# Joining small products and transposes on TensorE's queue in a two-block transformer kernel, and putting products of one PSUM bank ahead of its first reading

## The chip, the core and the metric

The kernel runs on one core of one Trainium2 chip. The metric is device time in microseconds of the whole program, the median of three runs. TensorE's clock has two levels, 1.2 and 2.4 GHz; the profile gives the granted share of the higher one.

## What is computed

Two transformer blocks one after the other on 256 tokens of width 1024, in float32. Cut to what matters here:

```
# first block, two layers l = 0, 1 (shared keys and values come in at l = 1)
proj = rmsnorm(h) @ w_in[l]                    # 768 columns "main", 256 "memory queries"
main_out = pool_mixer(main)          (l = 0)   # windowed means, then 4 groups of 192x192 weights
         = sliding_window_attn(...)  (l = 1)   # 12 heads of 64
mem_out  = softmax(q . mk) @ mv                # 4 heads of 64 over 256 memory rows
h += concat(main_out, mem_out) @ w_out[l]
h += relu(rmsnorm(h) @ w_up)**2 @ w_down       # 4096 wide
# second block
hq, hf, hi, hg, aq, ak, av, gl = split(rmsnorm(x) @ w_in)
y_hg = gated linear recurrence over time       # 8 heads of 128, within 128-token tiles by levels
y_at = causal attention with a bias            # 8 heads of 128
x += (gate0 * y_hg + gate1 * y_at) @ w_out;  x += silu-gated MLP(x)
```

## The kernel before

**Tiles.** The 256 tokens are two tiles `tt` of 128 rows. A weight product is three float32r products (high x high, high x low, low x high; tiles `wh`, `wl`, `xh`, `xl`), since weights and activations are split in a rounded part and a rest. In the rows `wh,xh` of 512 columns is such a product. What belongs to attention, pooling and the recurrence is done in plain float32; the profile records each plain product twice, so that "x4" of them are two products, and a transpose once.

**Order.** `Line` is a small planner in the kernel: every strand of work is a generator with a rank, which yields a latency in microseconds (or an event) whenever its next step must wait for another engine, and `Line.run` lets other strands, mostly weight products in pieces of six, fill the time. The framework's scheduler then places the instructions of each engine, keeps a bank's reader and the products written to the same bank apart by semaphores, and rotates four banks named `mm` and four named `acc`.

**The array's shapes.** A plain product whose contraction or output has 64 rows or fewer runs in a part of the array: in the profile `64*128` (64 rows contracted), `128*64` (64 output rows), `64*64` or `128*32` in place of `128*128`. Two products in different parts of the array can run side by side.

**Places that the change touches.** In stage mix0 (40 to 85 us of the span) `pool_mix` (line 917) multiplies six feature tiles `k` by `pool_w`, two tiles to a bank; feature tiles 1 and 4 take part in two groups, so each has 64-row products. `mem_attention` (line 867; also in stage mix1, 298 to 350 us) scores four heads, makes exponentials `me`, transposes them as two halves `i` (`exp_T`, line 441) and multiplies the copies `eT` by the memory values `mv`: a 64-row output each, half `i` in output rows 64i and on, both halves side by side. `Norm.into` (401) and `turned` (508) transpose a tile of 128 tokens as two halves of four transposes. In `mlp`, `turn` and `up_one` (564 to 575) do so for the hidden tile of one token tile. In the second block `on_q` and `diagonal` (1228 to 1247) make the 32x32 blocks on the diagonal, `recurrence` (1301) works by levels (`level`, line 1249: tile `fQ`, `fK`), `heads_T` and `heads_proj` (1370 to 1388) normalise and transpose four heads of queries or keys, and `score` in `attend` (1410) puts two heads' logits into one bank and reads each.

Of the kernel before, what the change touches and what calls it, by code (L numbers as in the profile page):

```python
# [8 lines left out]
F32 = mybir.dt.float32  # L9
# [6 lines left out]
P = 128  # L16
# [25 lines left out]
def kernel(  # L42
# [149 lines left out]
    def col(i, n=1):  # L192
        return cols[:, i:i + n]
# [189 lines left out]
    class Norm:  # L383
# [17 lines left out]
        def into(self, xs, tt, g, done):  # L401

            xn, lat = self.xn, 1.2
            if self.r is None:
                self.rstd()
                lat = 3.0
            else:
                xn = keep.tile([P, D], F32, tag="xn", name="xn", bufs=2)
            for c in range(2):
                V.tensor_scalar(xn[:, half(c)], self.src[:, half(c)], self.r, None, op0=ALU.mult)  # L410
            for c in range(2):
                yield lat
                split_T(xn[:, half(c)], xs, tt, 4 * c, 4, g[:, 4 * c:4 * c + 4])
                lat = 0.8
            done.at(2.0)
# [92 lines left out]
    def turned(xs, src, tt, g, done):  # L508

        for c in range(2):  # L510
            split_T(src[:, half(c)], xs, tt, 4 * c, 4, None if g is None else g[:, 4 * c:4 * c + 4])
            yield 1.3
        done.at(1.5)

    def add_turned(xs, g=None):

# [36 lines left out]
    def mlp(key, xs, there, nb, ku, hidden, finish, ends=1):  # L553
# [7 lines left out]
            for tt in range(TT):  # L561
                hT_there[b, tt] = Event()

        def turn(b, tt, y):
            yield 3.2
            split_T(y, hT[b], tt, 0, ku)
            hT_there[b, tt].at(5.1)

        def up_one(b, tt):

            if b not in hT:
                hidden_tiles(b)
            ps = mm_bank()
            yield from lin(ps, ktiles(xs, tt), W((key, "up", b)))
            line.add(-2, turn(b, tt, hidden(ps)))

        def up(b):
            hidden_tiles(b)
# [288 lines left out]
    def mem_attention(l, q, xs, tt, q_there, done):  # L867
# [20 lines left out]
        for i, ps in enumerate(pss):  # L888
# [8 lines left out]
            V.reciprocal(sm[:, 2 * i:2 * i + 2], sm[:, 2 * i:2 * i + 2])  # L897
            for hp in range(2):
                scaled(e[i][:, hp, :], sm[:, 2 * i + hp:2 * i + hp + 1])
        yield 3.2  # L900
        eTs = []
        for i in range(2):
            eTs.append(exp_T([e[i][:, hp, tok(c)] for hp in range(2) for c in range(2)]))
            yield 1.5
        po = by128(mm_bank())
        for hp in range(2):
            for c in range(2):
                for i in range(2):
# [8 lines left out]
    def pool_mix(xs, done):  # L917

        a, b = (act.tile([P, 6, S], F32, tag="win", name="win", bufs=2) for _ in range(2))
        prev = u  # L920
        for lev, (k0, s) in enumerate(((0, a), (1, b), (3, a), (4, b))):
            n = 1 << lev
            for eng, t0, t1 in ((V, k0, 5), (G, 5, 6)):
                if t0 < t1:
                    o = slice(t0, t1)
                    eng.tensor_copy(s[:, o, :n], prev[:, o, :n])
                    eng.tensor_tensor(s[:, o, n:], prev[:, o, n:], prev[:, o, :S - n], ALU.add)  # L927
            for k, p0, p1, g in PIECES:
                if g == lev:
                    r, w = s[p0:p1, k, :], WIN[g]  # L930
                    V.tensor_tensor(r[:, :w], r[:, :w], short[p0:p1, g, :w], ALU.mult)  # L931
                    V.scalar_tensor_tensor(u[p0:p1, k, :], r, 1.0 / w, u[p0:p1, k, :], op0=ALU.mult, op1=ALU.subtract)  # L932
            prev = s
        for k0 in range(0, 6, 2):
            yield 6.0 if k0 == 0 else 0
            ps = mm_bank().rearrange("p (k t) -> p k t", t=S)
            for k in (k0, k0 + 1):
                for t, q0, q1, g in PIECES:
                    if t != k:
                        continue  # L940
                    d0 = k * P + q0 - g * 192
                    src = [(t2, r0, r1) for t2, r0, r1, g2 in PIECES if g2 == g]
                    for i, (t2, r0, r1) in enumerate(src):
                        mm(ps[q0:q1, k - k0, :], pw[r0:r1, t2, d0:d0 + q1 - q0], u[r0:r1, t2, :],
                           i == 0, i == len(src) - 1)
                xh, xl = (t[:, k, :] for t in xs)
                A.activation(xh, ps[:, k - k0, :], AF.Copy, scale=col(V_PSCALE + k))
                V.scalar_tensor_tensor(xl, ps[:, k - k0, :], col(V_PSCALE + k), xh.bitcast(F32),
                                       op0=ALU.mult, op1=ALU.subtract)
        done.at(1.5)  # L950

    mem_kv = {0: add_mem_kv(0, 0, 6.0, accs1)}
# [266 lines left out]
    def on_f(c, hs, ps):  # L1219
        A.activation(fF[c][:, hs, :], ps, AF.Sigmoid)  # L1220
        A.activation(fK[c][:, hs, :], ps, AF.Sigmoid, scale=-1.0)
        for i in range(hs.start, hs.stop):
# [2 lines left out]
            V.tensor_scalar(f, f, olb[:, hd:hd + 1], lb[:, hd:hd + 1], op0=ALU.mult, op1=ALU.add)  # L1225
            V.tensor_scalar(k, k, olb[:, hd:hd + 1], None, op0=ALU.mult)

    def on_q(c, hs, ps):
        V.scalar_tensor_tensor(fQ[c][:, hs, :], ps, HG_SCALE, fF[c][:, hs, :], op0=ALU.mult, op1=ALU.mult)
        qs = b2([2, S], "qs")  # L1230
        A.activation(qs, ps, AF.Copy, scale=HG_SCALE)
        line.add(5, diagonal(c, hs, qs))

# [6 lines left out]
    def diagonal(c, hs, qs):  # L1240
        yield 1.5
        pd = mm_bank()[:, :128].rearrange("p (h t) -> p h t", t=32)
        for i in range(2):
            for tt in range(TT):
                quarters(pd[:, 2 * i + tt, :], fK[c][:, hs.start + i, tok(tt)], qs[:, i, tok(tt)], 32)
        V.tensor_tensor(AI[c][:, 2 * hs.start:2 * hs.stop, :], pd, own[:, None, :].to_broadcast([P, 4, 32]), ALU.mult)
        diag_done[c, hs.start].at(2.1)

    def level(m, c):
        def halves(t):  # L1250
# [38 lines left out]
                q = slice(32 * i, 32 * i + 32)  # L1289
                A.copy(at[q, :, q], AI[c][q])  # L1290

    diag_done = {(c, j): Event() for c in range(2) for j in (0, 2)}
    A_there, hv_there = events(), events()

    def gates_T(c):
# [3 lines left out]
        yield from head_chunk("hq", c, on_q)  # L1299

    def recurrence(c):
        yield [diag_done[c, 0], diag_done[c, 2]]
        for m in (1, 2, 4, 8, 16, 32, 64):
            level(m, c)
            yield 6.0
# [61 lines left out]
    q_there, k_there, v_there = events(), events(), events()  # L1367
    left = {}

    def heads_T(t, dst, scale, done):  # L1370

        y = head_norm(t, 4, P, b2([4, P], "hn"))
        yield 8.4
        pt = by128(mm_bank())
        for i in range(4):
            tr(pt[:, i, :], y[:, i, :])
        if scale is None:
            A.copy(dst, pt)
        else:
            A.activation(dst, pt, AF.Copy, scale=scale)  # L1380
        left[done] = left.get(done, 0) + 1
        if left[done] == 2:
            done.at(5.8)

    def heads_proj(key, c, tt, dst, scale, done):
        t = b2([4, P], "tm")
        A.copy(t, by128((yield from project((key, c), x2, tt))))
        line.add(9, heads_T(t, dst, scale, done))

    def attention_in():  # L1390
        for c in range(2):
# [10 lines left out]
    def attend(tt, xs, done):  # L1402
# [7 lines left out]
        def score(hp):  # L1410
            sc = scs[hp] = b2([2, S], "sc")
            ps = acc_bank().rearrange("p (h k) -> p h k", k=S)
            for i in range(2):
                hd = 2 * hp + i
                c = slice(hd, hd + 1)
                mm(ps[:, i, :nk], aq[tt][:, hd, :], ak[hd // 4][:, hd % 4, :nk])
                V.tensor_tensor_reduce(sc[:, i, :nk], ps[:, i, :nk], rel[hd // 4][:, hd % 4, k0:], 1.0, -3 * NEG,
                                       ALU.add, ALU.min, nm[:, c])
                A.activation(sc[:, i, :nk], sc[:, i, :nk], AF.Exp, bias=nm[:, c], scale=-1.0, accum_out=sm[:, c])
# [179 lines left out]
```

## Time and profile before

| | |
|---|---|
| median of three runs | 1031.24 us (1030.45 to 1032.26) |
| the profiled execution | 1031.49 us |
| its span, from first to last instruction | 1029.6 us |
| TensorE busy | 1022.1 us (99%) |
| TensorE's weight loads busy | 901.6 us (88%) |
| VectorE, ScalarE, GpSimd busy | 640.0, 565.4, 100.8 us |
| granted clock over the span | 1.000 |
| HBM read | 182.58 MB |

The median is 0.25 us below the profiled execution, whose time is 1.9 us more than its span. A TensorE record is longer than its share of the time, because products overlap in the array: what a product costs is the distance from its start to the next one's. Such starts are what the rows further down are used for.

### The profile page before, as it was taken

To read this page: it belongs to the slowest core of one execution; us is meant where nothing else is said; L and a number is where in the kernel's file an instruction comes from. 1 tells how busy PE (TensorE), PEld (TensorE's weight loads), DVE (VectorE), ACT (ScalarE), POOL (GpSimd) and SP (SyncE) were. 2 spreads that over 40 slices of the span, in tenths; PEclk is the share of its full clock that TensorE was granted. 3 is DMA by queue.
4 is the path that set the end of the run, shared out by engine and by line. 5 is a ranking of instruction groups with operands and counts; after the bars stand their busy time and mean duration, and the time that the engine had idled before them with its cause. 6 is when DMAs were issued, how large, how long until landed. Compare 5 with 4: busy or idle time off the path is not lost.

```text
span 1029.6 us, 18411 instructions
## 1 busy us (share of the span) xinstructions
PE 1022.1 (99%) x7353; PEld 901.6 (88%) x7353; DVE 640.0 (62%) x1002; ACT 565.4 (55%) x904; POOL 100.8 (10%) x143
## 2 busy tenths in 40 slices
PE   9999999999999999999999999999999999999998
PEld 8768999998876788899988988888999988999997
DVE  6976664565678765564576569847635766455553
ACT  6856544454678654444466455758744455444341
POOL 1524000000142000000000004330000000000000
PEclk9999999999999999999999999999999999999999
DMA  9854566556552269666557554334455566565741
GB/s 339 279 164 163 166 196 208 169 185 207 181 165 82 71 182 327 198 191 212 171 181 237 196 165 165 124 124 156 142 184 175 179 196 199 164 216 167 231 145 41
DMA packets 107765, 186.40 MB, mean 181 GB/s; under 512 B 6808, under 2 KB 31648, under 8 KB 107680
## 3 DMA queue, kind: packets, MB, share of 16 engines
q1 hardware_dynamic: 106160, 180.13, 53.8%
q0 software_dynamic: 1104, 4.80, 1.4%
q8 instruction: 57, 0.93, 0.4%
q10 hardware_dynamic: 416, 0.30, 0.1%
q14 instruction: 28, 0.23, 0.1%
HBM read 182.58 MB, written 2.63 MB: 180 GB/s over the span
## 4 chain that ended last, share of the span: by engine, by line
PE 94%; DVE 2%; DMA 2%; issue 1%; ACT 0%; ACTq 0%
PE acc L152 58%; PE mm L152 33%; PE mm L159 3%; DMA raw<-in_w_mem_kv_dram 1%; DVE wl L248 1%; DMA raw<-in_w_in_dram 1%; DMA raw_T<-in_xT_dram 0%; DVE wl L243 0%; DVE u L932 0%; DVE u L820 0%; DVE hs L427 0%; ACT xn L398 0%; DVE win L931 0%; ACT wh L247 0%; DVE win L927 0%
## 5 line engine op out<-in xcount | busy, mean ns | idle before, releaser
L243 DVE TENSOR_TENSOR wl<-raw,wh 128x1024 fp32r<-128x1024 f32 (+1 forms) x316 | 378.2, 1219 | 174.0 <-ACT wh L242 168.2
L242 ACT CAST wh<-raw 128x1024 fp32r<-128x1024 f32 (+1 forms) x316 | 322.5, 1045 | 171.9 <-PE acc L152 100.0
L152 PE MATMUL mm<-xh,wh 128*128 128x256 f32 x752 | 208.2, 277 | 0.0
L152 PE MATMUL mm<-xl,wh 128*128 128x256 f32 x752 | 207.8, 276 | 0.0
L152 PE MATMUL mm<-xh,wl 128*128 128x256 f32 x752 | 207.7, 276 | 0.0
L152 PEld LDWEIGHTS mm<-xh,wh 128*128 128x128 f32 x752 | 141.2, 188 | 1.4 <-issue 0.4
L152 PEld LDWEIGHTS mm<-xl,wh 128*128 128x128 f32 x752 | 141.3, 188 | 1.0
L152 PEld LDWEIGHTS mm<-xh,wl 128*128 128x128 f32 x752 | 141.2, 188 | 0.0
L152 PE MATMUL acc<-wh,xh 128*128 128x512 f32 x336 | 138.1, 411 | 0.0
L152 PE MATMUL acc<-wh,yl 128*128 128x512 f32 x342 | 134.7, 394 | 0.0
L152 PE MATMUL acc<-wl,yh 128*128 128x512 f32 x342 | 134.0, 392 | 0.0
L152 PE MATMUL acc<-wh,yh 128*128 128x512 f32 x342 | 133.4, 390 | 0.0
L152 PE MATMUL acc<-wh,xl 128*128 128x512 f32 x337 | 132.5, 394 | 0.0
L152 PE MATMUL acc<-wl,xh 128*128 128x512 f32 x336 | 132.1, 393 | 0.0
L152 PE MATMUL acc<-xh,wh 128*128 128x256 f32 x416 | 115.6, 278 | 0.7 <-ACT wh L242 0.7
L152 PE MATMUL acc<-xh,wl 128*128 128x256 f32 x416 | 115.2, 277 | 0.5 <-DVE wl L243 0.5
L152 PE MATMUL acc<-xl,wh 128*128 128x256 f32 x416 | 115.2, 277 | 0.0
L152 PEld LDWEIGHTS acc<-xh,wh 128*128 128x128 f32 x416 | 78.1, 188 | 1.2 <-ACT wh L242 1.1
L152 PEld LDWEIGHTS acc<-xh,wl 128*128 128x128 f32 x416 | 78.1, 188 | 0.9 <-DVE wl L243 0.9
L152 PEld LDWEIGHTS acc<-xl,wh 128*128 128x128 f32 x416 | 78.2, 188 | 0.2
L152 PEld LDWEIGHTS acc<-wl,yh 128*128 128x128 f32 x342 | 64.2, 188 | 13.7
L152 PEld LDWEIGHTS acc<-wh,xh 128*128 128x128 f32 x336 | 63.2, 188 | 14.8 <-issue 2.8
(240 smaller groups left out, 1283.0 us busy)
## 6 DMA issues: line engine op xcount, KB each, us to landing
raw<-in_w_in_dram SPq DMA_DIRECT2D x86, 512.0 KB, 4.7
raw<-in_w_up_dram SPq DMA_DIRECT2D x64, 512.0 KB, 4.7
raw<-in_w_down_dram SPq DMA_DIRECT2D x64, 512.0 KB, 4.8
raw<-in_w_out_dram SPq DMA_DIRECT2D x24, 512.0 KB, 4.8
raw<-in_w_ffn_gate_dram SPq DMA_DIRECT2D x44, 256.0 KB, 4.2
raw<-in_w_ffn_up_dram SPq DMA_DIRECT2D x44, 256.0 KB, 4.6
raw<-in_w_ffn_down_dram SPq DMA_DIRECT2D x22, 512.0 KB, 5.2
raw<-in_w_mem_kv_dram SPq DMA_DIRECT2D x8, 512.0 KB, 10.3
```

The lines of the kernel that those rows point to most:

```text
L152: PE.matmul(out_, lhsT, rhs, start=start, stop=stop)
L159: PE.transpose(out_, in_, ident)
L242: A.copy(wh[:, ks, :], raw[:, ks, :])
L243: V.tensor_sub(wl[:, ks, :], raw[:, ks, :], wh[:, ks, :].bitcast(F32))
L248: V.scalar_tensor_tensor(wl[:, k, :], raw[:, k, :], gk, wh[:, k, :].bitcast(F32), op0=ALU.mult, op1=ALU.subtract)
```

## The change

It moves instructions and adds none: as many products and transposes run on TensorE as before. The edits are these.

- `Norm.into`, `turned`: for token tile 0 the two halves are transposed one right after the other, without a pause for other work; for token tile 1 as before.
- `mlp`: the hidden tiles of two `up_one` calls are transposed together, after the second.
- `mem_attention`: both halves' exponentials are waited for (4.0 us in the plan, before 3.2) and transposed without a pause; among the value products half 1, whose copy is the later one, comes first.
- `pool_mix`: each feature tile has a bank of its own.
- `diagonal`: two pairs of heads go together into one bank, with one multiplication behind them.
- `heads_T`: two projections are normalised first and then transposed together.
- `attend.score`: both heads' products come ahead of the first reading of their bank.

```
@@ Norm.into
             for c in range(2):
-                yield lat
+
+                if tt or c == 0:
+                    yield lat if tt else lat + 0.8
                 split_T(xn[:, half(c)], xs, tt, 4 * c, 4, g[:, 4 * c:4 * c + 4])
@@ turned
             split_T(src[:, half(c)], xs, tt, 4 * c, 4, None if g is None else g[:, 4 * c:4 * c + 4])
-            yield 1.3
-        done.at(1.5)
+            if tt:
+                yield 1.3
+        done.at(2.8 if tt == 0 else 1.5)
@@ mlp
-        def turn(b, tt, y):
+        ys = []
+
+        def turn(ys):
             yield 3.2
-            split_T(y, hT[b], tt, 0, ku)
-            hT_there[b, tt].at(5.1)
+            for b, tt, y in ys:
+                split_T(y, hT[b], tt, 0, ku)
+                hT_there[b, tt].at(5.1)
...
-            line.add(-2, turn(b, tt, hidden(ps)))
+            ys.append((b, tt, hidden(ps)))
+            if len(ys) == 2:
+                line.add(-2, turn(ys[:]))
+                ys.clear()
@@ mem_attention
-        yield 3.2
+        yield 4.0
         eTs = []
         for i in range(2):
             eTs.append(exp_T([e[i][:, hp, tok(c)] for hp in range(2) for c in range(2)]))
-            yield 1.5
+        yield 1.5
         po = by128(mm_bank())
         for hp in range(2):
             for c in range(2):
-                for i in range(2):
+
+                for i in (1, 0):
@@ pool_mix
-        for k0 in range(0, 6, 2):
-            yield 6.0 if k0 == 0 else 0
-            ps = mm_bank().rearrange("p (k t) -> p k t", t=S)
-            for k in (k0, k0 + 1):
...
+        for k in range(6):
+            yield 6.0 if k == 0 else 0
+            ps = mm_bank()[:, :S]
...
@@ on_q, diagonal
-        line.add(5, diagonal(c, hs, qs))
+        qss.append((hs, qs))
+        if len(qss) == 2:
+            line.add(5, diagonal(c, qss[:]))
+            qss.clear()
...
-        V.tensor_tensor(AI[c][:, 2 * hs.start:2 * hs.stop, :], pd, own[:, None, :].to_broadcast([P, 4, 32]), ALU.mult)
-        diag_done[c, hs.start].at(2.1)
+        V.tensor_tensor(AI[c], pd, own[:, None, :].to_broadcast([P, 8, 32]), ALU.mult)
+        diag_done[c].at(2.1)
@@ heads_T, heads_proj
-        line.add(9, heads_T(t, dst, scale, done))
+        ys.append((head_norm(t, 4, P, b2([4, P], "hn")), dst, done))
+        if len(ys) == 2:
+            line.add(9, heads_T(ys[:], scale))
+            ys.clear()
@@ attend.score
             for i in range(2):
                 hd = 2 * hp + i
+                mm(ps[:, i, :nk], aq[tt][:, hd, :], ak[hd // 4][:, hd % 4, :nk])
+            for i in range(2):
+                hd = 2 * hp + i
                 c = slice(hd, hd + 1)
-                mm(ps[:, i, :nk], aq[tt][:, hd, :], ak[hd // 4][:, hd % 4, :nk])
                 V.tensor_tensor_reduce(sc[:, i, :nk], ps[:, i, :nk], rel[hd // 4][:, hd % 4, k0:], 1.0, -3 * NEG,
```

How this moves instructions shows on TensorE's queue at three places. In the order's rows the shape is that of the output; names are the tiles (written <- read).

**Stage mix1, around the memory attention of token tile 0** (`me` exponentials, `mv` memory values, `skT`/`qT`, `sc`, `sv` sliding-window scores, weights and values). Before:

```order
L152 MATMUL mm<-eT,sv 64x128 x2
L159 MATMUL mm<-ident,me 128x128 x2
L152 MATMUL acc<-skT,qT 128x128 x2
L159 MATMUL mm<-ident,me 128x128 x2
L152 MATMUL acc<-wh,xl 128x512
L152 MATMUL acc<-skT,qT 128x128 x2
L152 MATMUL mm<-eT,mv_581 64x128
L159 MATMUL mm<-ident,sc 128x128 x4
L152 MATMUL acc<-skT,qT 128x256 x2
L152 MATMUL acc<-skT,qT 128x128
L152 MATMUL mm<-eT,mv_581 64x128 x7
L159 MATMUL mm<-ident,sc 128x128 x2
```

and now:

```order
L159 MATMUL mm<-ident,me 128x128 x4
L152 MATMUL mm<-eT,sv 64x128 x2
L152 MATMUL acc<-skT,qT 128x128 x2
L152 MATMUL acc<-wh,xl 128x512
L152 MATMUL acc<-skT,qT 128x128 x2
L152 MATMUL acc<-skT,qT 128x256 x2
L152 MATMUL mm<-eT,mv_581 64x128 x8
L159 MATMUL mm<-ident,sc 128x128 x4
L152 MATMUL acc<-skT,qT 128x128 x2
L159 MATMUL mm<-ident,pj 128x128 x2
L159 MATMUL mm<-ident,sc 128x128 x2
```

The eight value products on `mv`, one and seven before, stand together, the eight transposes of `me` lie closer, and the single scores on `skT` have come together in pairs.

**Stage mix0, the pooling products** (`u` pooled inputs, `pw` weights, `mkT`/`mqT` memory scores; each `mm` number is a bank). Before:

```order
L152 MATMUL mm_736<-u_92,pw_96 128x256 x2
L152 MATMUL mm_771<-u_92,pw_96 128x256 x2
L152 MATMUL acc_749<-mkT0_571,mqT_596 128x256
L152 MATMUL acc_750<-mkT0_571,mqT_596 128x256
L152 MATMUL acc_749<-mkT0_571,mqT_596 128x256
L152 MATMUL acc_750<-mkT0_571,mqT_596 128x256
L152 MATMUL mm_780<-u_92,pw_96 64x256 x4
L152 MATMUL acc_804<-mkT0_571,mqT_660 128x256 x2
```

and now:

```order
L152 MATMUL mm_736<-u_92,pw_96 128x256 x2
L152 MATMUL mm_765<-u_92,pw_96 64x256 x2
L152 MATMUL acc_743<-mkT0_571,mqT_596 128x256
L152 MATMUL acc_744<-mkT0_571,mqT_596 128x256
L152 MATMUL acc_743<-mkT0_571,mqT_596 128x256
L152 MATMUL acc_744<-mkT0_571,mqT_596 128x256
L152 MATMUL mm_765<-u_92,pw_96 64x256 x2
L152 MATMUL mm_772<-u_92,pw_96 128x256 x2
L152 MATMUL mm_777<-u_92,pw_96 128x256 x2
L152 MATMUL acc_814<-mkT0_571,mqT_660 128x256 x2
```

Feature tiles 0 and 2, which had the banks 736 and 771 and stood next to each other, are parted: tile 1 (bank 765) and the scores come between them.

**Stage mix0, the memory attention of token tile 0 behind them.** Before:

```order
L159 MATMUL mm<-ident,me 128x128 x4
L159 MATMUL mm<-ident,ks 128x128 x2
L152 MATMUL acc<-mkT_571,mqT 128x256
L152 MATMUL acc<-wh,xh 128x512
L152 MATMUL acc<-wl,xh 128x512
L152 MATMUL acc<-wh,xl 128x512
L159 MATMUL mm<-ident,me 128x128 x4
L152 MATMUL mm<-eT,mv_572 64x128
L152 MATMUL acc<-wh,xh 128x512
L152 MATMUL acc<-wl,xh 128x512
L152 MATMUL acc<-wh,xl 128x512
```

and now:

```order
L159 MATMUL mm<-ident,me 128x128 x4
L152 MATMUL acc<-wh,xl 128x512
L152 MATMUL acc<-wh,xh 128x512
L152 MATMUL acc<-wl,xh 128x512
L152 MATMUL acc<-wh,xl 128x512
L159 MATMUL mm<-ident,me 128x128 x4
L159 MATMUL mm<-ident,ks 128x128 x2
L152 MATMUL acc<-wh,xh 128x512
L152 MATMUL acc<-wl,xh 128x512
L152 MATMUL acc<-wh,xl 128x512
L152 MATMUL mm<-eT,mv_572 64x128 x8
```

The value products come eight at a time, three weight products after the second half's transposes; before, one came at once and the other seven eighteen weight products later.

## Rows read from the trace of the kernel before

**Rows 1.** The page: busy time by engine, and the clock in 40 slices

```profile
PE 1022.1 (99%) x7353; PEld 901.6 (88%) x7353; DVE 640.0 (62%) x1002; ACT 565.4 (55%) x904; POOL 100.8 (10%) x143
...
PEclk9999999999999999999999999999999999999999
```

**Rows 2.** Waits of PE: waiter <- releaser: us in total, times, longest

```profile
PE mm L159 <- POOL ks L435: 1.1, 1, 1.1
...
PE mm L152 <- issue: 0.5, 1, 0.5
...
PE mm L152 <- DVE u L932: 0.2, 1, 0.2
```

**Rows 3.** Timeline of PE near 84 us: start us, record us, instruction, xcount

```profile
84.33 0.40 PE L152 MATMUL acc<-wh,xl 128*128 128x512 f32 x1
84.56 0.60 PE L159 MATMUL mm<-ident,h 128*128 128x128 f32 x4
...
85.23 0.40 PE L152 MATMUL acc<-wl,xh 128*128 128x512 f32 x1
```

**Rows 4.** Timeline of PE near 777 us, eight transposes in a row

```profile
776.76 1.03 PE L159 MATMUL mm<-ident,ho 128*128 128x128 f32 x8
...
777.75 0.28 PE L152 MATMUL acc<-xl,wh 128*128 128x256 f32 x1
```

**Rows 5.** Timeline of PE near 301 us, two products in parts of the array

```profile
300.59 0.40 PE L152 MATMUL acc<-wh,xl 128*128 128x512 f32 x1
300.91 0.49 PE L152 MATMUL acc<-skT,qT 64*128 64x128 f32 x4
...
301.67 0.39 PE L152 MATMUL acc<-wl,xh 128*128 128x512 f32 x1
```

**Rows 6.** Timeline of PE from 318 us, in stage mix1

```profile
318.65 0.43 PE L152 MATMUL mm<-eT,mv 128*64 128x128 f32 x2
319.01 0.66 PE L159 MATMUL mm<-ident,sc 128*128 128x128 f32 x4
319.59 0.92 PE L152 MATMUL acc<-skT,qT 64*128 64x256 f32 x6
320.44 1.09 PE L152 MATMUL mm<-eT,mv 128*64 128x128 f32 x14
321.46 0.44 PE L159 MATMUL mm<-ident,sc 128*128 128x128 f32 x2
321.83 0.48 PE L152 MATMUL acc<-skT,qT 64*128 64x128 f32 x2
```

**Rows 7.** Timeline of PE at 338 us: eight value products together

```profile
338.31 1.09 PE L152 MATMUL mm<-eT,mv 128*64 128x128 f32 x16
```

**Rows 8.** Timeline of PE near 652 us: the level of 32 rows, each half

```profile
650.81 1.10 PE L152 MATMUL mm<-fQ,fK 128*32 128x32 f32 x32
651.83 0.50 PE L152 MATMUL acc<-wh,xh 128*128 128x512 f32 x1
...
653.41 1.10 PE L152 MATMUL mm<-fQ,fK 128*32 128x32 f32 x32
```

**Rows 9.** Timeline of PE near 700 us, the logits of two heads

```profile
699.81 0.39 PE L152 MATMUL acc<-wh,xl 128*128 128x512 f32 x1
...
700.93 0.47 PE L152 MATMUL acc<-ak,aq 128*128 128x128 f32 x2
...
702.49 0.40 PE L152 MATMUL acc<-wl,xh 128*128 128x512 f32 x1
```

**Rows 10.** Timeline of PE near 64 us: one 64-row product of 256 columns alone

```profile
64.29 0.70 PE L152 MATMUL acc<-mkT,mqT 64*128 64x256 f32 x2
64.92 0.50 PE L152 MATMUL acc<-wh,xh 128*128 128x512 f32 x1
```

**Rows 11.** Timeline of ACT near 65 us

```profile
64.53 0.61 ACT L448 COPY eT<-mm 128x512 f32<-128x512 f32 x1
...
66.36 1.10 ACT L242 CAST wh<-raw 128x1024 fp32r<-128x1024 f32 x1
```

More of the change, by code (lines that the diff above doesn't have):

```diff
@@ L933, in pool_mix @@
             prev = s
-        for k0 in range(0, 6, 2):
-            yield 6.0 if k0 == 0 else 0
-            ps = mm_bank().rearrange("p (k t) -> p k t", t=S)
-            for k in (k0, k0 + 1):
[L938 to L949, printed above, removed]
+        for k in range(6):
+            yield 6.0 if k == 0 else 0
+            ps = mm_bank()[:, :S]
+            for t, q0, q1, g in PIECES:
+                if t != k:
+                    continue
+                d0 = k * P + q0 - g * 192
+                src = [(t2, r0, r1) for t2, r0, r1, g2 in PIECES if g2 == g]
+                for i, (t2, r0, r1) in enumerate(src):
+                    mm(ps[q0:q1, :], pw[r0:r1, t2, d0:d0 + q1 - q0], u[r0:r1, t2, :], i == 0, i == len(src) - 1)
+            xh, xl = (t[:, k, :] for t in xs)
+            A.activation(xh, ps, AF.Copy, scale=col(V_PSCALE + k))
+            V.scalar_tensor_tensor(xl, ps, col(V_PSCALE + k), xh.bitcast(F32), op0=ALU.mult, op1=ALU.subtract)
         done.at(1.5)
@@ L1226, in on_f @@
             V.tensor_scalar(k, k, olb[:, hd:hd + 1], None, op0=ALU.mult)
+    qss = []
     def on_q(c, hs, ps):
@@ L1238, in quarters, with diagonal @@
             mm(ps[32 * i:32 * i + 32], keys[:, 32 * i:32 * i + 32], queries[:, n * i:n * i + n])
-    def diagonal(c, hs, qs):
+    def diagonal(c, qss):
         yield 1.5
[L1242 to L1245, printed above, removed]
-        V.tensor_tensor(AI[c][:, 2 * hs.start:2 * hs.stop, :], pd, own[:, None, :].to_broadcast([P, 4, 32]), ALU.mult)
-        diag_done[c, hs.start].at(2.1)
+        pd = mm_bank()[:, :256].rearrange("p (h t) -> p h t", t=32)
+        for hs, qs in qss:
+            for i in range(hs.start, hs.stop):
+                for tt in range(TT):
+                    quarters(pd[:, 2 * i + tt, :], fK[c][:, i, tok(tt)], qs[:, i - hs.start, tok(tt)], 32)
+        V.tensor_tensor(AI[c], pd, own[:, None, :].to_broadcast([P, 8, 32]), ALU.mult)
+        diag_done[c].at(2.1)
     def level(m, c):
@@ L1290, in level @@
                 A.copy(at[q, :, q], AI[c][q])
-    diag_done = {(c, j): Event() for c in range(2) for j in (0, 2)}
+    diag_done = events()
     A_there, hv_there = events(), events()
@@ L1301, in recurrence @@
     def recurrence(c):
-        yield [diag_done[c, 0], diag_done[c, 2]]
+        yield diag_done[c]
         for m in (1, 2, 4, 8, 16, 32, 64):
@@ L1368, with heads_T @@
     left = {}
-    def heads_T(t, dst, scale, done):
-        y = head_norm(t, 4, P, b2([4, P], "hn"))
+    ys = []
+    def heads_T(ys, scale):
         yield 8.4
[L1374 to L1383, printed above, removed]
+        for y, dst, done in ys:
+            pt = by128(mm_bank())
+            for i in range(4):
+                tr(pt[:, i, :], y[:, i, :])
+            if scale is None:
+                A.copy(dst, pt)
+            else:
+                A.activation(dst, pt, AF.Copy, scale=scale)
+            left[done] = left.get(done, 0) + 1
+            if left[done] == 2:
+                done.at(5.8)
     def heads_proj(key, c, tt, dst, scale, done):
```

## The prediction

> **What bounds the kernel now.** I read the page's busy times first: TensorE is busy for 1022.1 of 1029.6 us, and its granted clock is full in every slice, so it is at 2.4 GHz throughout [rows 1]. Then the waits of PE: the longest are about 1 us each and happen once, among them 1.1 us for GpSimd's keys, 0.2 for a pooled input and 0.5 with no releaser that the profile shows [rows 2]. So nothing that another engine does faster can help. Only two things can: fewer nanoseconds between the starts of TensorE's own instructions, or one of those small waits. As no instruction is added or removed, I read on in the timeline of PE, start against start, for what position costs.
>
> **Prices of a position.** A weight product of 512 columns costs 0.23 (84.33 to 84.56). Four transposes cost 85.23 - 84.56 - 0.23 = 0.44, that is 0.11 each, and no more for coming between weight products [rows 3]. Eight in a row cost 777.75 - 776.76 = 0.99 less one product of 256 columns at half of 0.23, so 0.88: twice four [rows 4]. A stay in a part of the array is another matter. From 300.59 to 301.67 lie one weight product before it, the stay and one after: 1.08 - 2 x 0.23 = 0.62. The two products in it run side by side, two passes of 128 columns at 0.11 each, 0.22 in all; 0.40 is left for leaving the full array and coming back, 0.2 for each change of shape [rows 5]. With only transposes between two stays the return is cheaper: 0.58 from 319.01 to 319.59 for four of them, 0.14 more than 0.44 [rows 6].
>
> A product that stands alone takes as long as two side by side: the record of a score pair is 0.49 and that of one score 0.48 [rows 5, 6], and seven value products, of which one is alone, take 1.09 as eight do [rows 6, 7].
>
> Over the whole order TensorE changes its shape 96 times before and 89 times now. That, and which products stand alone, is nearly all the change is.
>
> **Part by part.**
>
> *Joined transposes* (norms, turned tiles, hidden tiles, heads): about a dozen fours become eights. Eight cost twice four [rows 3, 4], so I take nothing. What covers a first half that now waits for the second is the weight products behind it; nobody consumes a half before the event that both set.
>
> The transposes bring a rule into play. In the stretch around the eight transposes of the output heads the clock shows no fall; all 40 slices are full [rows 1, 4]. The Trainium skill ("TensorE: Matmul & The Clock Gate", section "PE-mode transpose") says that transposes do not count as busy to the clock's monitor as other products do, which speaks against lengthening such stretches. By the row the joining costs 0. By the Trainium skill's page it could cost clock, and I keep that as a rival.
>
> *Memory attention in mix1.* One value product stood alone for 0.36 (318.65 to 319.01) before seven took 1.02 (320.44 to 321.46); eight take what the seven do [rows 6, 7]: -0.36. Among the scores around it, two stays held one lone product each: 0.85 for two of 256 columns and one of 128, and 0.41 for the single one (taken as a pair's 1.08 - 0.23 - 0.43, since the records are alike). Two pairs of 128 columns stood beside them at 0.42 each. Now there are two stays of 0.42 and one with a pair of each width, 0.42 + 0.43 = 0.85: 1.69 for 2.10, -0.41. One return fewer is -0.14. Together **-0.9**.
>
> *mix0, the value products.* The same split in both token tiles: 2 x -0.36 = -0.72, and two changes of shape fewer (24 to 22) at 0.14 to 0.2 each: -0.35.
>
> *mix0, pooling.* With a bank each the feature tiles need not wait for a reader, and the 0.2 for a pooled input goes, because that product now stands later [rows 2]. But the 64-row products of tiles 0 and 2, which ran as a pair, come apart, and so does another of them that ran beside a score. A lone 64-row product of 256 columns costs 0.63 with its changes of shape [rows 10], 0.43 of which are its two passes. Twice 0.43 is +0.86, less the -0.2: **+0.66**.
>
> *New waits at the value products.* They now come three (token tile 0) or eight weight products behind the second half's transposes, and the very first needs the later copy. ScalarE's copy takes 0.61 and, where a cast of weights stands ahead of it, 1.10 more [rows 11], 1.71 in all. Three weight products and two transposes are 0.9, eight weight products 1.8. Beside the cast ScalarE has exponentials and other copies in its queue there. No row shows this wait. Its bounds are 0 (copies ahead of time, as TensorE met them before) and 1.2 for each token tile (1.71 and half of another cast, less 0.9). I take 0.3 each, nearer to the lower end, since before the change TensorE waited nowhere for `eT`: **+0.6**. Who is late then is TensorE itself, and all behind it.
>
> So mix0 gives -0.72 - 0.35 + 0.66 + 0.6 = **+0.2**.
>
> *Diagonal blocks and levels.* The four diagonal groups already stood in one stretch; two banks fewer change nothing on the path. But the two halves of the level of 32 rows, six weight products apart, now follow each other. Each stay took 1.02 and the stretch between them 1.58 (651.83 to 653.41), of which six products explain 1.38 [rows 8]. The 0.2 goes, and with it about half of one stay's changes, 0.1: -0.3. Transposes directly behind a level return at 0.14 instead of 0.2 in two places: -0.1. Together **-0.4**.
>
> *Logits.* From 699.81 to 702.49 lie five weight products (1.15) and two products of each width (2 x 0.22 + 2 x 0.44 = 1.32), 2.47 of 2.68 [rows 9]. The 0.21 are two waits for VectorE to leave a bank. Of the eight second products four came that soon after the first; the others stood behind enough weight products. Four at 0.1: **-0.4**. Between 0 and -0.8 all is possible. The first reading starts 0.1 to 0.2 later, which weight products cover.
>
> DMA queues, POOL and SP issue the same transfers in the same order.
>
> **The sum:** 0 - 0.9 + 0.2 - 0.4 - 0.4 = -1.5 us. Against the profiled execution of 1031.49 that is 1030.0; against the median, 0.25 lower, **1029.7**. A measurement of this kernel tells a change of about 0.2% (2.06 us) from none, so the likeliest result is faster by less than that.
>
> **Rivals.**
>
> 1. *All of it and more.* The new waits stay away (-0.6) and the stall of 0.5 to 0.7 without a releaser inside a level [rows 2], which may depend on where code lies, goes too: -2.1 to -2.8, 1028.4 to 1029.1, faster. For it: TensorE met no such wait before. Against: the code is as long as ever. 0.22.
> 2. *Given back.* Waits for the copies in mix0 and mix1, 0.4 to 0.5 at each of the four places, take the 1.5: within 0.5 us of no change, 1031.2. For it: the planner's latencies were set so that work arrived just in time, and now stand closer. 0.20.
> 3. *The copies become the bound (slower).* One mechanism: at the four places TensorE, in order, stands before the first value product until ScalarE has cast, exponentiated and copied. From 0.5 each it decides the sign; at 1.1 each, near the upper bound, the change is -1.5 - 0.6 + 4.4 = +2.3, 1033.5. For it: ScalarE's 1.71 is longer than the 0.9 that covers it in one of the four [rows 11]. Against: the other three have 1.8 and more. 0.08, over half of it by more than 0.2%.
> 4. *Transposes do have an entry price.* If each of a dozen joined groups saved 0.14, as a return from a stay does, the sum were -1.5 - 1.7 = -3.2, 1028.0. The rows speak against it: joining leaves 0.01 [rows 3, 4]. 0.03.
> 5. *The clock falls.* If eight transposes in a row let the clock fall to 1.2 GHz, weight products would cost about double for a while. To end slower by 0.2%, 3.6 us would have to be lost, 0.3 at each of a dozen places. All slices are at full clock with two such eights among them [rows 1, 4]. 0.02. It would be the Trainium skill's rule on transposes ("TensorE: Matmul & The Clock Gate") at work; the trace so far shows no harm from it.
>
> That the change does not do what it says is excluded for TensorE by its order.
>
> **How the numbers follow.** The forecast has 0.45. Its own spread is -0.7 to -2.3 us from the logits (0 to -0.8) and the waits (0 to 1.2 each), and a fifth of it, 0.09, lies beyond -2.06. Faster by over 0.2%: 0.09 + 0.22 + 0.03 = 0.34, less 0.01 for the part of rival 1 that lies just short of 2.06: 0.33. Slower: 0.05 of rival 3 and 0.02 of rival 5, 0.07. The same: the rest, 0.60. The range leaves out 2 in 10: down to 1028.2 it takes most of rival 1, up to 1031.9 rival 2.
>
> **What would show it.** In mix0 and mix1 the value products as four groups of x16 of about 1.02, and no lone x2. Waits "mm <- ACT eT" at them: none for rival 1, 0.3 for the forecast, 1 and more for rival 3. In pooling, the span from the first pooled product to the first `me` longer by about half a microsecond. The level of 32 rows as one stay of x64. Logits as x4 without a weight product between. Transposes as x8 of 0.88. I am wrong if the stages not named move by more than 0.3 us, if a new wait of PE exceeds 1 us, or if the clock shows less than full.

## The result, and the profile after

The changed kernel takes 1038.40 us (median of 4 runs, 1036.57 to 1039.68) against 1031.57 (1030.45 to 1032.26) for the kernel before: the ratio of the runs is 1.0051, 95% interval 1.0026 to 1.0076 (the two medians alone give 1.0066). Forecast were 1029.7, a range of 1028.2 to 1031.9, and 1033.5 for the rival that was slower. The change is slower by 0.5 to 0.7%, and the time lies outside the range.

The profiled execution of the changed kernel took 1036.57 us, 5.08 more than that of before. It is the fastest of the four: what the others took beyond it does not show in its rows. The page, busy time by engine and the clock in 40 slices:

```profile
PE 1025.8 (99%) x7353; PEld 908.6 (88%) x7353; DVE 640.8 (62%) x1000; ACT 562.4 (54%) x902; POOL 102.7 (10%) x143
...
PEclk9999999999999999999999999999999999999999
```

Against [rows 1], TensorE is busy for 3.7 us more with the same 7353 instructions, at the same clock. So most of this loss is not idle time: the same products take longer. The rest is in the waits of PE (waiter <- releaser: us in total, times, longest):

```profile
PE mm L152 <- ACT eT L450: 1.9, 1, 1.9
PE mm L159 <- POOL ks L437: 1.1, 1, 1.1
...
PE acc L152 <- DVE s L1049: 0.5, 1, 0.5
PE mm L152 <- issue: 0.3, 1, 0.3
```

Two are new: 1.9 for ScalarE's `eT` and 0.5 for VectorE's reading of a score. The 0.2 for `u` of [rows 2] is gone, as forecast.

**Where it went.** At some places both kernels have started exactly the same products and transposes. The difference of TensorE's start there is what has been lost until then:

| start before | start after | difference | lost or gained since the line above | forecast |
|---|---|---|---|---|
| 46.96 | 46.17 | -0.80 | ahead of the first edit: executions differ there | |
| 66.25 | 66.03 | -0.22 | pooling +0.58 | +0.66 |
| 75.27 | 74.11 | -1.16 | value products in mix0 -0.94 | -1.07, +0.6 for waits |
| 88.44 | 87.14 | -1.30 | -0.14 | 0 |
| 262.85 | 264.36 | +1.51 | first feed-forward part **+2.81** | 0 |
| 316.47 | 317.79 | +1.32 | -0.19 | 0 |
| 321.46 | 323.64 | +2.18 | mix1, scores and values **+0.86** | -0.9 |
| 339.50 | 343.70 | +4.21 | mix1, wait for `eT` **+2.03** | 0 |
| 564.28 | 568.55 | +4.27 | +0.06 | 0 |
| 604.63 | 610.48 | +5.85 | projections of the second block **+1.58** | 0 |
| 655.95 | 660.87 | +4.92 | levels -0.93, about -0.4 of it at the level of 32 rows | -0.4 |
| 711.37 | 716.08 | +4.71 | logits -0.21 | -0.4 |
| 873.13 | 877.77 | +4.64 | -0.07 | 0 |
| 888.83 | 893.98 | +5.14 | last feed-forward part **+0.50** | 0 |

What the prediction worked out mostly came: the value products of mix0, the level of 32 rows and the logits gain about 1.6 us, and pooling costs 0.6. Of the other half of the -0.93, 0.24 is a stall without a releaser inside a level, 0.53 long before and 0.29 here; over the kept profiles it is 0.2 to 1.5, so that part is luck. Three stretches that it had at nothing cost 4.9, and mix1 2.9.

**The same products, longer.** In the table of windows (from:to in us, length, PE busy and instructions, granted clock, DMA share, GB/s) of the changed kernel the first row spans 96 products of 256 columns, from the start of the first to the start of the product behind them, the second row 384, the third 94:

```profile
128.67:139.98 11.31, 11.31 (x98) 1.00 0.53 180
...
565.61:610.84 45.23, 45.23 (x386) 1.00 0.58 197
877.77:888.84 11.07, 11.07 (x95) 1.00 0.35 113
```

and the same stretches in the kernel before (here the third has 96, as two of its products come earlier in the changed kernel):

```profile
129.77:140.67 10.90, 10.90 (x97) 1.00 0.55 187
...
561.43:604.97 43.54, 43.54 (x385) 1.00 0.60 204
872.89:883.80 10.91, 10.91 (x98) 1.00 0.46 146
```

That is 11.31 / 96 = 117.8 ns for a product in place of 113.5, at a clock of 1.00 in both, without a wait in between; the third row gives 11.07 / 94 = 117.8 too. The kernel has two speeds for one stream, and no long stream of the kept profiles settles between them. In the changed kernel 48 + 6 x 96 = 624 products of the first feed-forward part run at the long step: 624 x 4.3 ns = 2.7 of the 2.81. The 384 of the second block give 45.23 - 43.54 = 1.69. Products of 512 columns keep their mean of 0.229.

**Mix1.** The timeline of PE (start us, record us, instruction, xcount, idle before and its releaser):

```profile
318.69 0.49 PE L152 MATMUL acc<-skT,qT 64*128 64x128 f32 x4
319.11 0.49 PE L152 MATMUL acc<-wh,xl 128*128 128x512 f32 x1
319.53 1.63 PE L152 MATMUL acc<-skT,qT 64*128 64x128 f32 x8
321.09 1.09 PE L152 MATMUL mm<-eT,mv 128*64 128x128 f32 x16
322.12 0.66 PE L159 MATMUL mm<-ident,sc 128*128 128x128 f32 x4
322.70 0.49 PE L152 MATMUL acc<-skT,qT 64*128 64x128 f32 x2
323.64 0.49 PE L152 MATMUL acc<-skT,qT 64*128 64x128 f32 x2 [0.45 <-DVE s L1049]
...
332.06 0.40 PE L152 MATMUL acc<-wh,xl 128*128 128x512 f32 x1
334.39 0.44 PE L152 MATMUL mm<-eT,sv 128*64 128x128 f32 x4 [1.94 <-ACT eT L450]
```

The eight value products take 322.12 - 321.09 = 1.03 as foreseen, where one and seven took 0.36 + 1.02 [rows 6]. The scores are another matter. The stay with a pair of each width takes 321.09 - 319.53 = 1.56, not 0.85: the two products of 256 columns do not run side by side. The last pair comes apart too, 324.12 - 322.70 = 1.42 for 0.42, and there the profile names the reason: VectorE reads a score (`s`) out of its bank so late that TensorE stands for 0.45. The first has the same reason, though no idle time shows, because the record of the product before covers the wait. Each score has an `acc` bank of its own, there are four, and VectorE's readings of them are these:

```profile
319.49 0.35 DVE L1049 CUSTOM_DVE_ANT_0 sc<-acc,bias,nsink 128x128 f32<-128x128 f32 x1
...
320.06 0.35 DVE L1049 CUSTOM_DVE_ANT_0 sc<-acc,bias,nsink 128x128 f32<-128x128 f32 x1
```

In the trace the wait that the profile names ends 62 ns after such a reading (323.579 to 323.641). The two products of 256 columns start at 319.897 and 320.469, 62 and 63 ns after the ends of the two readings shown (319.835 and 320.406). In the kernel before they started 7 ns apart, at 319.594 and 319.601. So they too start when a bank has been read, and not side by side.

Later, at 332.9, TensorE stands for `eT`. ScalarE's timeline there:

```profile
328.37 1.05 ACT L242 CAST wh<-raw 128x1024 fp32r<-128x1024 f32 x1
331.78 0.56 ACT L904 ACTIVATE me<-acc,ms,mr 128x256 f32<-128x256 f32 x1 [2.37 <-DVE ms L900]
...
333.42 0.57 ACT L904 ACTIVATE me<-acc,ms,mr 128x256 f32<-128x256 f32 x1
333.87 0.21 ACT L904 ACTIVATION_READ_ACCUMULATOR me<-acc,ms,mr 128x1 f32 x1
333.96 0.86 ACT L450 COPY eT<-mm 128x256 f32<-128x256 f32 x2
```

The transposes that this `eT` copies begin at 330.39 on TensorE and are over some 0.6 later. Yet ScalarE, which works in order, has four exponentials of the memory softmax of the other token tile ahead of the copy, and the first of those waits 2.37 for VectorE's maxima. The copy is not for the memory values `mv` but for the sliding window's `sv`, which the change does not touch.

**What came out as forecast.** The value products in mix0, without a wait ahead of them (the 0.33 from a weight product's start to theirs is the product and its change of shape):

```profile
65.70 0.40 PE L152 MATMUL acc<-wh,xl 128*128 128x512 f32 x1
66.03 1.09 PE L152 MATMUL mm<-eT,mv 128*64 128x128 f32 x16
...
71.96 0.39 PE L152 MATMUL acc<-wh,xl 128*128 128x512 f32 x1
72.28 1.09 PE L152 MATMUL mm<-eT,mv 128*64 128x128 f32 x16
```

The level of 32 rows as one stay, 1.84 for 2 x 1.02 [rows 8], and the logits of two pairs of heads, 1.54 with the weight product behind them:

```profile
659.03 1.91 PE L152 MATMUL mm<-fQ,fK 128*32 128x32 f32 x64
660.87 0.50 PE L152 MATMUL acc<-wh,xh 128*128 128x512 f32 x1
...
705.04 1.47 PE L152 MATMUL acc<-ak,aq 128*128 128x128 f32 x8
706.16 0.58 PE L152 MATMUL acc<-wh,xh 128*128 128x512 f32 x1
706.58 0.40 PE L152 MATMUL acc<-wl,xh 128*128 128x512 f32 x1
```

With four more weight products (0.92) this is 2.46 for the 2.68 of [rows 9]. And eight transposes joined cost what two fours do (0.87 for those at 83.29); the clock is full in every slice, so no harm to it behind a joined group is to be seen.

### The profile page after: what moved, and what is told of

It is laid out like the page before. It is cut to its first block, busy times and chain, and to the rows that moved or that the text cites. A ratio compares the mean times of both kernels' runs of the same rounds, so it can differ in the third digit from the quotient of the medians.

```text
span 1034.7 us, 18408 instructions
## 1 busy us (share of the span) xinstructions
PE 1025.8 (99%) x7353; PEld 908.6 (88%) x7353; DVE 640.8 (62%) x1000; ACT 562.4 (54%) x902; POOL 102.7 (10%) x143
## 4 chain that ended last, share of the span: by engine, by line
PE 96%; POOL 1%; issue 1%; DVE 0%; DMA 0%; ACT 0%; SPq 0%; POOLq 0%; ACTq 0%
PE acc L152 59%; PE mm L152 34%; PE mm L159 3%; DMA raw<-in_w_in_dram 0%; POOL hs L348 0%; POOL win L937 0%; ACT me L904 0%; POOL win L936 0%; DVE u L829 0%; POOL st L421 0%; POOL mr L348 0%; POOL ks L437 0%; DVE wl L243 0%; POOL st L348 0%; DVE ms L900 0%
## 5 line engine op out<-in xcount | busy, mean ns | idle before, releaser
L152 PEld LDWEIGHTS acc<-wh,yh 128*128 128x128 f32 x342 | 64.3, 188 | 13.6 <-ACT yh L370 0.2
L152 PEld LDWEIGHTS acc<-wh,yl 128*128 128x128 f32 x342 | 64.4, 188 | 13.3
```

What stands on the lines that cost most here:

```text
L152: PE.matmul(out_, lhsT, rhs, start=start, stop=stop)
```

## The experiments

Theory S: joined transposes put the stream behind them into the long step, and the memory attention's edit brings the wait for `eT`. Rivals: the long step belongs to waits or code position (W), to each execution (L), or to the place in a cycle of the stream at which the group meets it (P). All runs, with the kernel before on the same chip; the stretches are those of 96 and of 384 products, from the one profiled execution of each:

| kernel | median us (range) | ratio to before, 95% interval | 96 take, us | 384 take, us | `eT` wait, us |
|---|---|---|---|---|---|
| the change, again | 1039.37 (1037.87 to 1039.59) | 1.0055 to 1.0081 | 11.30 | 45.22 | 1.9 |
| e1 hidden tiles apart | 1035.79 (1034.35 to 1036.44) | 1.0025 to 1.0050 | 10.90 | 45.22 | 1.9 |
| e2 norms, turned tiles apart | 1038.57 (1038.23 to 1038.88) | 1.0052 to 1.0078 | 11.31 | 45.23 | 1.9 |
| e3 no joined transposes | 1034.60 (1033.14 to 1035.86) | 1.0013 to 1.0033 | 10.90 | 43.55 | 1.9 |
| e4 memory attention as before | 1035.91 (1034.27 to 1036.78) | 1.0022 to 1.0047 | 11.31 | 45.23 | none |
| e5 before + hidden tiles | 1037.41 (1035.76 to 1039.80) | 1.0040 to 1.0068 | 11.31 | 45.23 | none |
| e6 pooling, diagonal, logits alone | 1031.51 (1030.84 to 1034.43) | 0.9990 to 1.0008 | 10.90 | 43.54 | none |
| e7 before + memory attention | 1034.58 (1032.45 to 1035.83) | 1.0014 to 1.0032 | 10.91 | 43.55 | 1.9 |
| e8 mix0, diagonal, logits | **1029.85** (1029.03 to 1031.80) | 0.9972 to 0.9992 | 10.90 | 43.54 | none |
| e9 as e5, nine for eight | 1034.59 (1034.32 to 1037.66) | 1.0019 to 1.0047 | 10.91 | 45.22 | none |
| e10 before, five for four | 1035.41 (1033.81 to 1039.55) | 1.0024 to 1.0049 | 10.90 | 45.22 | none |
| e11 memory attention, yields alone | 1034.44 (1032.76 to 1038.46) | 1.0019 to 1.0045 | 10.91 | 43.54 | 1.9 |

**e1, the hidden tiles apart** (`mlp` as before, all else changed):

```
-            for b, tt, y in ys:
-                split_T(y, hT[b], tt, 0, ku)
+            split_T(y, hT[b], tt, 0, ku)
```

> The changed kernel with its hidden tiles transposed one by one again, as before. Theory S (eight transposes in a row inside a stream of 256-column products leave that stream in a slower step, 117.7 instead of 113.3 ns, until something else interrupts it): the stretches from 111 to 251 us and from 877 to 889 us go back to 113.3 ns, that is 2.7 and 0.7 us; the one from 565 to 611 us stays slow. The median falls from 1038.4 by 3.4 or more (more if other executions have the second feed-forward part slow too), to 1035 or less. Theory W (the slow step has to do with the order of waits or the place of the code, and the eights only happen to stand there): no change, 1037 to 1039, the stretches still at 117.7 ns.

```profile
129.28:140.18 10.90, 10.90 (x97) 1.00 0.55 184
...
563.69:608.91 45.22, 45.22 (x385) 1.00 0.58 196
```

The first stretch went back, the second did not, as S has it; the last part also did (10.90 for 96). The median fell by 2.6 from the first runs of the change, by 3.6 from its second ones, where 3.4 or more was expected.

**e2, norms and turned tiles apart:**

```
-                if tt or c == 0:
-                    yield lat if tt else lat + 0.8
+                yield lat
```

> The changed kernel with the transposes of the normalised and turned tiles as before (two fours apart). Theory S: the stretch from 565 to 611 us (384 products of 256 columns) goes back to 113.3 ns, 1.7 us; the one from 111 to 251 us stays slow, since the hidden tiles still come as eights. Median 1038.4 - 1.7 = 1036.7. Theory W: the stretch from 565 to 611 us stays at 117.7 ns, 1038.4.

The 384 products stay at 45.23. S in this simple form fell: the eights just ahead of them are not what does it.

**e3, every joined group of transposes undone** (`mlp`, `Norm.into`, `turned`, `heads_T`):

> The changed kernel with every joined group of transposes undone (hidden tiles, norms, turned tiles, heads); pooling, memory attention, diagonal blocks and logits as changed. Theory S: no slow stretch but the short ones that the kernel before has too; 1038.4 - 5 or more, 1031 to 1033: what is left is the gain of the other edits (2.5) against the two waits in stage mix1 (2.0 and 0.5). Theory W: slow stretches somewhere, 1035 or more.

```profile
129.40:140.30 10.90, 10.90 (x97) 1.00 0.57 185
...
565.43:608.98 43.55, 43.55 (x386) 1.00 0.61 205
```

Both long stretches are gone, so joining the transposes is what brought them here. But 1034.60 is 1.6 over the expected. Its profile has a fall of the clock behind the wait for `eT` (below, at the repeated run) and 1.3 in the stall inside a level. That is not all: the executions with a mean clock of 0.998 take 1033.14 to 1035.75, those at 1.000 take 1033.25 to 1035.86, so the clock does not part them.

**e4, the memory attention as before** (yields of 3.2 and 1.5 each, halves 0, 1):

> The changed kernel with the memory attention as before (waits and order of the halves). If the 2.0 us wait of TensorE for ScalarE's eT at 332 us and the 0.5 for VectorE's s at 323 us come from this edit, both go: -2.5, less the 0.9 it gains there and 0.9 in mix0: 1038.4 - 0.7 = 1037.7. If they come from the shifted plan (other strands) instead, the wait stays and only the gains are lost: 1040. Theory S says nothing of the slow stretches here: they stay.

Both waits in mix1 went, so the edit brought them; 1035.91 is less than the 1037.7 that the waits' length alone gives. All seven executions have a mean clock of 1.000.

**e5, the joined hidden tiles alone on the kernel before:**

> The kernel before with one edit alone: the hidden tiles transposed as eights. Theory S: the first feed-forward part (stretch from about 113 to 250 us) and the last one's first stretch near 875 us go to 117.7 ns, 2.7 and 0.7 us: 1031.6 + 3.4 = 1035.0; the recurrence's projections (384 products near 563 us) stay at 113.3. Theory W (it takes the shifted times of the other edits): no change, 1031.6, all stretches at 113.3 ns.

```profile
129.34:140.65 11.31, 11.31 (x98) 1.00 0.51 176
...
563.59:608.82 45.23, 45.23 (x385) 1.00 0.57 195
877.39:888.07 10.68, 10.68 (x96) 1.00 0.38 128
```

One small edit, and the kernel is 0.54% slower. (The third row has 94 products, 113.6 ns each.) S was right on the first stretch and wrong on the other two: the projections near 563 us, 180 us behind the last joined hidden tile ahead of them, run at the long step, and the last part does not. The streams from 397 us on, behind a second joined pair at 379 us, do not either.

**e6, pooling, diagonal blocks and logits alone:**

> The changed kernel without joined transposes and with the memory attention as before: pooling, diagonal blocks and logits alone are left. No slow stretch and no wait for eT in mix1. By the drift seen so far pooling is +0.6, levels and diagonal blocks -0.3 to -0.7, logits -0.2: 1031.6 - 0.3 to +0.1, 1031.3 to 1031.7, the same as before. If the waits in mix1 stay, they do not come from the memory attention's edit: 1033.5 or more.

1031.51, as expected. No long stretch, no wait for `eT`. The level of 32 rows stays in two halves here, although the diagonal blocks are joined.

**e7, the memory attention's edit alone:**

> The kernel before with the memory attention's edit alone. Theory M (the edit brings the order in which ScalarE's copies of eT stand behind the exponentials of the memory softmax in mix1): the 1.9 us wait for eT near 330 us and 0.5 for s are there, -0.9 in mix0, -0.5 in mix1: 1031.6 + 1.0 = 1032.6. Rival C (it takes the other edits' shift too): no wait over 0.3, 1031.6 - 1.4 to -1.8 = 1030.

Theory M: both waits are there without any other edit. The time is 2.0 us longer than expected: the five executions with a mean clock of 0.998 or less take 1034.86 to 1035.83, the five others 1032.45 to 1034.31.

**The change once more:**

> The changed kernel itself once more. Theory S with the slow step a property of the program's order: the same stretches are at 117.7 ns as in the first profile (111 to 251, 565 to 611, 877 to 889 us). Theory L (a lottery of each execution): other stretches are slow this time, or none. Time 1036.5 to 1039.7 either way.

The same eight streams are at the long step as in the first profile, so L fell for them: two executions of one program agree. An execution can still matter elsewhere: the times at a full clock scatter (e10: 1033.81 and 1039.55, both 1.000), and each kernel has one or two profiles. This profile, 2.70 us longer than the first, tells where part of the time of e3 and e7 went. Windows of 1 us behind the wait for `eT` (same columns):

```profile
333.00:334.00 1.00, 0.00 (x0) 1.00 0.96 363
...
335.00:336.00 1.00, 1.00 (x14) 1.00 0.00 0
336.00:337.00 1.00, 1.00 (x10) 0.54 0.00 0
337.00:338.00 1.00, 1.00 (x7) 0.50 0.00 0
338.00:339.00 1.00, 1.00 (x6) 0.50 0.07 16
339.00:340.00 1.00, 1.00 (x6) 0.75 0.00 0
```

TensorE did nothing from 332.9 to 334.9; a microsecond after it began again its granted clock fell to 0.50, the lower level of 1.2 GHz, and stayed there for 3.4 us: transposes of 0.11 took 0.21. Against the first profile of the same program this costs 1.53 (it is 0.46 later at the start behind the wait, 1.99 later when the clock is full again). Of the seven profiles with the 1.9 us wait four show the fall (this one, e2, e3, e7) and three do not (the first, e1, e11). The Trainium skill ("TensorE: Matmul & The Clock Gate", section "HAM oscillation — how this bites in real kernels") tells of a kernel whose waits for DMA put the clock at half for each tile. The trace agrees that a wait can do it; but the one of 1.9 us did it in four profiles of seven only. Two further falls stand in the profiles of e8 and e9, of 3.4 and 6.8 us, behind waits of 1.3 and 1.1 us for a pooled input `u` near 54 us; behind the equally long wait for `ks` (1.1, in eleven profiles) and the stall inside a level there is none. The rest of the 2.70 are 0.45 ahead of 47 us and 0.74 in that stall, 0.3 in one and 1.0 in the other.

**e8, what the rows spoke for:** on the kernel before, the memory attention's edit for layer 0 alone (mix0), diagonal blocks and logits:

```
+        yield 3.2 if l else 4.0
...
+                for i in ((0, 1) if l else (1, 0)):
```

> The kernel before with what the rows spoke for: the memory attention's edit in the first block's layer 0 alone (mix0), the diagonal blocks and the logits; pooling, transposes and the memory attention of layer 1 as before. Theory: -0.9 to -1.3 in mix0, -0.3 to 0 at the levels, -0.3 at the logits, no wait for eT in mix1 and the 256-column stretches at 113.3 ns: 1031.8 - 1.5 = 1030.3. Rival (the place in the order decides and a stretch falls into the slow step by the shift): 1032 to 1035, with a stretch at 117.7 ns.

1029.85 against 1031.43, ratio 0.9982, interval 0.9972 to 0.9992: faster than both kernels. Between the points that stand at 63.54 and 75.61 us in the kernel before, where the value products of mix0 lie, it gains 1.35. Its profile, 1030.68, is one of the slower executions: it has the wait of 1.3 for `u` and the fall of the clock just named, which costs some 1.5. The level of 32 rows stays in two halves, as in e6, so the diagonal blocks show no gain there.

**e9, nine transposes for eight,** the last of each pair of hidden tiles done twice (work added):

```
+            PE.transpose(pt[:, i, :], src[:, i * P:(i + 1) * P], ident)
```

> As e5_only_hidden, but the last transpose of each pair is done twice (nine in a row in place of eight, the last MLP five in place of four): the same instructions otherwise. Theory N (a long group of transposes brings the slow step): the stretches from 112 to 252 us and at 563 us stay at 117.7 ns, 1037.4 + 0.3. Theory P (where in its cycle the group meets the stream of products decides; its length matters only by the time it takes): some of the stretches change their speed, 1033 to 1036 with the first part back at 113.3.

```profile
131.91:142.82 10.91, 10.91 (x98) 1.00 0.53 183
...
563.72:608.94 45.22, 45.22 (x385) 1.00 0.59 196
```

One transpose more, and the first feed-forward part is back at 113.6 ns; the kernel is 2.8 us faster than e5 for doing more. N fell. The last part's first stream, short in e5, is at the long step here: 11.19 for 95.

**e10, five for four in the kernel before** (the same line, for every hidden tile; work added):

> The kernel before, with the last transpose of each hidden tile done twice (five in a row for four, three for two). Theory N: no group longer than before's eights, all stretches stay at 113.3 ns, 1031.8 + 1.2 (twelve transposes at 0.11) = 1033.0 at most. Theory P: one or more stretches go to 117.7 ns without any joining, 1034 or more.

```profile
129.24:140.14 10.90, 10.90 (x97) 1.00 0.54 183
...
561.46:606.68 45.22, 45.22 (x385) 1.00 0.58 197
```

Nothing was joined, and the 384 products run at the long step. So P: neither eights nor length matter as such, a change in what precedes can turn a stretch.

The starts in the traces, in whole nanoseconds, show the cycle. In most stretches the products of 512 columns repeat three steps, 226, 229 and 232 ns; which of a weight's three products has which step differs from place to place and from kernel to kernel. In the 14 kept profiles 364 unbroken streams of 36 or more products of 256 columns follow directly on one of 512. In 44 of them the step just ahead of the stream was 226 to 228 ns, and these run at 117.8 ns to their end. In the other 320 it was 230 ns or more, and these begin with three to five products of some 118 ns and settle at 113.3. There is no exception. The place in the code, one half of W, does not decide by itself: the streams at 129.77 before and 128.67 in the changed kernel have the same 736 products and transposes ahead of them.

**e11, the yields of the memory attention without the order of its halves:**

> The kernel before with half of the memory attention's edit: the two halves of exponentials are waited for and transposed together (4.0 in the plan), but the value products keep their order. If the longer wait shifts the plan so that the softmax of the other token tile comes ahead of the copy of eT, the 1.9 us wait near 330 us is there: 1034 to 1035, as e7_only_memory without the gain at the value products. If the order of the halves is what does it: no such wait, 1031.8 to 1032.

```profile
PE mm L152 <- ACT eT L448: 1.9, 1, 1.9
```

The wait is there: the longer, joined wait of the plan moves the softmax of the other token tile ahead of the copy, as in the change (in ScalarE's timeline four exponentials from 329.33, the first after a wait of 2.37, then the copy at 331.51). The order of the halves does not bring the wait, and it carries the gain: without it mix0 gains nothing between 66 and 76 us.

## Why the prediction was wrong

**The step that failed first** is "Eight cost twice four [rows 3, 4], so I take nothing". The eight do cost twice four. What failed is the price of the weight products behind them, taken as one number for the whole kernel (half of 0.23). It has two values, 113.5 and 117.8 ns, and with the joined groups 624 + 384 + 94 products went to the longer one: +2.81, +1.58 and +0.50 in the table, 4.9 us together, where the profile lost 5.1 in all. Which of the two a stream gets goes with the step of a cycle at which it begins (under e10). The rivals had a clock that falls, at a dozen places; no rival had the same clock and a longer step. The trace of before did hold the sign: its long streams begin with a few products of 118 ns, and near 721 us, behind a pair of logits, its own products of 256 columns stay there:

```profile
720.99 0.47 PE L152 MATMUL acc<-xl,wh 128*128 128x256 f32 x1
721.30 0.28 PE L152 MATMUL acc<-xh,wl 128*128 128x256 f32 x1
...
724.83 0.28 PE L152 MATMUL acc<-xh,wl 128*128 128x256 f32 x1
724.96 0.60 PE L152 MATMUL mm<-eT,av 128*128 128x128 f32 x4
```

From 721.30 to 724.96 lie 31 products: 3.66 / 31 = 118 ns.

**Memory attention in mix1**, "-0.9": the value products gave the -0.36. The -0.41 for scores was taken from side-by-side pairs without asking whether a bank was free for each product: 1.69 forecast for all stays, 0.42 + 1.56 + 1.42 = 3.40 measured.

**New waits.** "I take 0.3 each" at the value products on `mv` was wrong in both directions: there is none there, and one of 1.9 elsewhere. Rival 3 had the right engine and the right order (casts, exponentials, copies on ScalarE) but looked only at the tiles that the edit names. e4, e7 and e11 show that the edit's yields bring it, the longer one and the one that went from between the halves; they are not told apart. What the prediction did not price is the clock after the wait, 1.53 where it falls. By its own numbers the upper bound of these waits is 1.71 + 0.55 - 0.9 = 1.36, not 1.2; the forecast does not hang on it.

**Right:** pooling (+0.58 for +0.66), the value products of mix0 (-0.94 for -1.07 without waits), the level of 32 rows (about -0.4, as forecast). The logits gave half: -0.21 for -0.4. The level's gain does not come from the diagonal blocks alone: its halves follow each other in the change, e1, e2 and e4, where the heads' transposes are joined, and stand apart in e3, e6 and e8, where of the two edits only that of the diagonal blocks is made. So of the terms e8 keeps -1.07 - 0.4 = -1.47 without waits; it measures 1029.85 - 1031.43 = -1.58.

**Not settled:** what inside TensorE makes the two steps, and how a given order puts a stream on one place of the cycle; that the order of waits shifts it is not excluded. Shown is that two profiles of the change agree in every long stream, that one transpose more turns a stream (e9, e10), and that the place in the cycle goes with the step without exception. An execution can shift the cycle too: between 619 and 653 us, behind the stall inside a level, the two profiles of the change stand at different places of it, where no long stream lies. e5, e10 and e11 also scatter by 4 to 6 us among executions, more than the two effects in their profiles explain.

## What to carry to other kernels

A kernel in which one engine is busy for 99% still has prices that hang on order: before costing an edit at nothing, measure the step of the longest streams, start against start, in the trace of before, and look for a second value. When a planned wait is lengthened, look at what it lets pass on every in-order queue, above all copies for work that the edit does not name. And take a bundle of edits apart on the chip: here three of them, that of the memory attention in mix0 alone, are faster by 1.6 us together (e8), while joined hidden tiles alone cost 5.5 (e5) and the memory attention alone 2.7 (e7).

## What was not expected of the hardware

The same stream of products of 256 columns runs at 113.5 or 117.8 ns at a granted clock of 1.00, for hundreds of products, and a single transpose more in each joined group ahead of it changes which (e5 against e9). Which one goes with the step of the 512-column product just ahead: 226 to 228 ns in all 44 long ones, 230 or more in all 320 short ones. A wait of 1.9 us can halve the clock for 3.4 us, a microsecond after work resumes, or not, in executions of one program.
